# Gate steps between the halves of up steps, a gate evacuation in six VectorE steps, and two gaps between tiles

## The chip, the cores and the metric

The kernel runs on one core of one Trainium2 chip. The metric is the device time of one execution in microseconds. The median of three timed runs is 2343.71 us (2341.99 to 2345.11); the execution that was profiled took 2340.65 us.

## The reference

Two decoder layers over 256 positions of width 2048 in float32, and a final RMSNorm. Each layer runs four groups of attention heads, adds their merged projection, and then the dense SwiGLU block, in which the change lies:

```python
for l in range(DEPTH):                                   # DEPTH = 2
    x = x + hybrid_mixer(rms_norm(x, attn_norm[l]), w_in[l], ...)
    h = rms_norm(x, ffn_norm[l])                         # 256 x 2048
    x = x + (jax.nn.silu(h @ w_gate[l]) * (h @ w_up[l])) @ w_down[l]   # hidden width 5632
return rms_norm(x, final_norm)
```

## The kernel before

**Numbers.** float32 operands are split into a high part, rounded to the type that TensorE takes at full rate, and the rest. A product is then three matmuls: high x high, high x rest, rest x high. `XS[i]` holds both parts of the normed x (two of the sixteen row blocks of 128 each), `wh` and `wl` those of the weights. `load` (L230) takes one unit of weights, 128 x 2048, from HBM into `raw` (one DMA on SP's queue, three buffers), and splits it in two halves of 1024 columns: ScalarE writes `wh` (L239), VectorE subtracts it to `wl` (L240). There are six buffers of `wh` and six of `wl`, each of 1024 columns.

**A layer's feed-forward part** runs over eleven blocks `g` of 512 hidden columns. `gate_up(g)` makes four steps for up and four for gate, in turns: u0 g0 u1 g1 u2 g2 u3 g3, each over a quarter of the 2048 rows and with one unit of weights. An up step (`ProjV.step`) is 24 matmuls of 512 columns at L256, x stationary, weights moving, into one of the two accumulators of the pool `accp` (`acc`, two banks of PSUM each). In block 0 the gate is a `ProjV` as well and takes the other accumulator. In blocks 1 to 10 the gate is a `ProjSW`: seven products in place of eight, from sums of the weights' quarters (`w_sum`, L350 to L355 on VectorE, split at L354, L356 to L358) and sums of x (`sums`, built once a layer, in the pool `qp`). Such a step is 42 matmuls of 256 columns (L371 to L373) and uses four pairs of the weight buffers; its seven results lie in the four banks of the pool `attp` (`att`). `out` (L375) adds them up: one step on ScalarE and seven on VectorE. Then Silu on ScalarE (L802; L798 in block 0) and, on VectorE, the product with up (L803), which is the last reader of up's accumulator.

**Around a block.** `turn` transposes the block's hidden values on TensorE (L813) through two `att` banks into `h` tiles. `down(c, p)` multiplies eight of these tiles by 256 columns of `w_down` (16 x a matmul of 512 columns and one of 256) in an accumulator and adds the result to X in two VectorE steps (`add_to`, L281 and L282), the second of which frees the accumulator. Blocks 0 and 1 have no down projections behind them, blocks 2 to 9 have four, block 10 has eight. `turn` of an even block comes in the program after the first of them, of an odd one after the last; of blocks 0 and 1 after the first up step of the block that follows.

**Order.** The program gives each engine's instructions; a planner orders them with its own durations, so VectorE's and ScalarE's steps of several units lie mixed, and `tc.issue_after` is the means to hold an order.

**Addresses.** `GAP_X`, `GAP_W`, `GAP_H` and `GAP_Q` are dead tiles, of so many times 32 bytes of each partition, ahead of `XS`, the weight buffers, the `h` tiles and the pool `qp`.

Of the kernel before, what the change touches and what calls it, by code (L numbers as in the profile page):

```python
# [8 lines left out]
F32 = mybir.dt.float32  # L9
# [6 lines left out]
S = 256  # L16
# [12 lines left out]
NG = HID // 512  # L29
GAP_X, GAP_W, GAP_H, GAP_Q = 1, 3, 1, 1  # L30

# [85 lines left out]
def pack_weights(w_in, w_uq, w_ukv, w_out, w_gate, w_up, w_down):  # L117
    us = []
    for l in range(DEPTH):
# [39 lines left out]
        for g in range(NG):  # L159
            for i in range(4):  # L160
                us += [up(g, i), unit(w_gate[l], 4 * i, 4, 0, 512) if g == 0 else gate(g, i)]
            for c, ps in down_after(g):
                us += dn(8 * c, 8, ps)
# [19 lines left out]
def trunk(ctx: ExitStack, tc: tile.TileContext, x_d, w_d, sm_d, c_d, out_d):  # L183
# [124 lines left out]
    class ProjV:  # L308
        def __init__(self, src, nk):
            self.acc, self.src, self.nk = Acc(), src, nk  # L310
            self.out = [self.acc.t[:, t].rearrange("p a b -> p (a b)") for t in range(2)]

        def step(self, k0):
            blk = load()
            for kk in range(4):
                x = self.src(k0 + kk)
                wh, wl = blk(kk * 512, 512)
                last = k0 + kk == self.nk - 1
                for t in range(2):
                    ts = slice(t * 128, t * 128 + 128)  # L320
                    self.acc.mm(t, self.out[t], x[:, 0, ts], wh, False)
                    self.acc.mm(t, self.out[t], x[:, 0, ts], wl, False)
                    self.acc.mm(t, self.out[t], x[:, 1, ts], wh, last)
# [7 lines left out]
    class ProjSW:  # L331
# [3 lines left out]
        def banks(self):  # L335
            ps = [attp.tile([128, 2, S], F32, name="att") for _ in range(4)]
            self.p = {1: ps[0][:, 0], 2: ps[0][:, 1], 3: ps[1][:, 0], 6: ps[2][:, 0],
                      7: ps[2][:, 1], 5: ps[3][:, 0], 4: ps[3][:, 1]}

        def step(self, k0):  # L340
# [3 lines left out]
            for j in range(2):  # L344
# [14 lines left out]
                a, b = slice(0, 128), slice(128, 256)  # L359
                x, y = XS[i], self.sums[i]  # L360
                for n, xh, xl, wh, wl, o in (
# [4 lines left out]
                        (7, y[:, 2, 0, :], y[:, 2, 1, :], ht, lt, 256),  # L366
                        (5, y[:, 0, 0, :], y[:, 0, 1, :], ht, lt, 0),
                        (4, x[:, 1, 0, b], x[:, 1, 1, b], ht, lt, 768)):
                    p, c = self.p[n], slice(o, o + 256)
                    first = i == 0 and n in (1, 3, 6, 5)  # L370
                    P.matmul(p, xh, wh[:, c], start=first, stop=False, skip_group_check=True)  # L371
                    P.matmul(p, xl, wh[:, c], start=False, stop=False, skip_group_check=True)  # L372
                    P.matmul(p, xh, wl[:, c], start=False, stop=i == 7, skip_group_check=True)  # L373

        def out(self):  # L375
            p = self.p
            c = [tp.tile([128, 512], F32, name="ff_g", tag="t2", bufs=T2) for _ in range(2)]
            c11, c12, c21, c22 = c[0][:, :256], c[0][:, 256:], c[1][:, :256], c[1][:, 256:]
            A.activation(c11, p[1], AF.Copy)
            V.tensor_add(c12, c11, p[6])  # L380
            V.tensor_add(c11, c11, p[2])
            V.tensor_add(c21, c12, p[7])
            V.tensor_sub(c12, c12, p[5])
            V.tensor_add(c12, c12, p[3])
            V.tensor_sub(c22, c21, p[5])
            V.tensor_add(c21, c21, p[4])
            return c
# [178 lines left out]
    for l in range(DEPTH):  # L566
# [214 lines left out]
        def gate_up(g, turn_last):  # L781
            up = ProjV(xk, KT)
            gate = ProjV(xk, KT) if g == 0 else ProjSW(sums)
            for i in range(4):
                up.step(4 * i)
                if i == 0 and turn_last is not None:
                    turn_last()
                gate.step(4 * i)
            if g == 0:
# [94 lines left out]
```

## Time and profile before

| | |
|---|---|
| median of three runs | 2343.71 us |
| profiled execution | 2340.65 us |
| its span, first to last instruction | 2338.8 us |
| TensorE busy | 2256.6 us, 96% |
| VectorE busy | 1834.7 us, 78% |
| ScalarE busy | 1256.3 us, 54% |
| up steps, v and block 0's gate (weights over x) at L256 | 2880 matmuls of 512 columns |
| gate steps of blocks 1 to 10 at L371 to L373 | 3360 matmuls of 256 columns |

Matmuls overlap: the duration of one holds a tail that runs beside the next one, so the rate is read from the time of a number of matmuls, or from differences of durations of one shape. In the names, `acc<-wh,XS` is a matmul into `acc` with `wh` moving and `XS` stationary. PEclk is the granted clock as a share of 2.4 GHz.

### The profile page before, as it was taken

What the parts mean: (1) busy time and instruction counts of PE and PEld (TensorE: products, weight loads), DVE (VectorE), ACT (ScalarE), POOL (GpSimd) and SP (SyncE); (2) the same over time, 40 slices, a digit from 0 to 9 for tenths busy, and PEclk for the clock granted to TensorE, in tenths of its full rate; (3) what the DMA queues carried; (4) which work ended last, traced back from release to release, by engine and by line L of the source; (5) the groups of instructions that cost most, each with busy time, mean ns of one, the idle gap of its engine ahead of it and who ended that gap; (6) DMA issues with size and microseconds to landing.
All of it is one profiled execution on the core that took longest, in us unless ns stands there. A gap on an engine that the chain in (4) does not pass through costs nothing.

```text
span 2338.8 us, 34343 instructions
## 1 busy us (share of the span) xinstructions
PE 2256.6 (96%) x13678; PEld 2007.8 (86%) x13678; DVE 1834.7 (78%) x2639; ACT 1256.3 (54%) x1629; POOL 0.2 (0%) x4
## 2 busy tenths in 40 slices
PE   8999999999999999999999999999999999999997
PEld 8888889788888888888998988897888888888887
DVE  8876767798888888778877865778887888887775
ACT  7454556654455544445564654666644445544454
POOL 0000000000000000000000000000000000000000
PEclk9999999999999999999999999999999999999999
DMA  7544445455455455455555344454544455444452
GB/s 294 185 151 178 154 149 206 159 192 187 180 198 198 172 178 186 168 187 198 186 184 189 138 168 158 166 202 159 190 172 180 179 198 198 171 172 174 174 209 90
DMA packets 61648, 419.88 MB, mean 180 GB/s; under 512 B 6832, under 2 KB 7088, under 8 KB 14768
## 3 DMA queue, kind: packets, MB, share of 16 engines
q1 hardware_dynamic: 61344, 417.63, 49.7%
q8 instruction: 107, 1.75, 0.3%
q14 instruction: 53, 0.43, 0.0%
q10 hardware_dynamic: 144, 0.07, 0.0%
HBM read 415.57 MB, written 2.10 MB: 179 GB/s over the span
## 4 chain that ended last, share of the span: by engine, by line
PE 93%; DVE 3%; ACT 2%; DMA 1%; issue 0%; ACTq 0%; DVEq 0%; SPq 0%
PE acc L256 70%; PE att L373 5%; PE att L371 5%; PE att L372 5%; PE att L256 4%; DVE wl L240 1%; ACT wh L239 1%; PE att L813 1%; DMA raw<-in_w_dram 1%; PE att L494 1%; DVE X L282 0%; PE att L484 0%; PE att L495 0%; PE att L503 0%; DMA X<-in_x_dram 0%
## 5 line engine op out<-in xcount | busy, mean ns | idle before, releaser
L239 ACT ACTIVATE wh<-raw 128x1024 fp32r<-128x1024 f32 (+1 forms) x650 | 663.6, 1027 | 744.2 <-PE acc L256 600.9
L240 DVE TENSOR_TENSOR wl<-raw,wh 128x1024 fp32r<-128x1024 f32 (+1 forms) x650 | 764.8, 1183 | 317.8 <-ACT wh L239 312.2
L256 PE MATMUL acc<-h,wh 128*128 128x512 f32 (+1 forms) x1824 | 629.1, 390 | 52.1 <-DVE X L282 52.1
L256 PE MATMUL acc<-wh,XS 128*128 128x512 f32 x1920 | 620.9, 397 | 8.4 <-ACT ff_g L798 8.4
L256 PE MATMUL acc<-h,wl 128*128 128x256 f32 x1744 | 499.9, 287 | 0.0
L256 PEld LDWEIGHTS acc<-h,wh 128*128 128x128 f32 x1824 | 345.6, 192 | 123.7 <-issue 53.4
L256 PEld LDWEIGHTS acc<-wh,XS 128*128 128x128 f32 x1920 | 362.5, 189 | 92.1 <-ACT ff_g L798 8.5
L256 PE MATMUL acc<-XS,wh 128*128 128x512 f32 (+1 forms) x1344 | 376.6, 347 | 6.3 <-ACT XS L435 6.3
L256 PE MATMUL acc<-wl,XS 128*128 128x512 f32 x960 | 381.1, 397 | 1.0 <-DVE wl L240 1.0
L256 PEld LDWEIGHTS acc<-h,wl 128*128 128x128 f32 x1744 | 337.8, 194 | 0.2
L256 PE MATMUL acc<-XS,wl 128*128 128x256 f32 x1056 | 299.1, 283 | 0.0
L256 PEld LDWEIGHTS acc<-XS,wh 128*128 128x128 f32 x1344 | 233.6, 189 | 38.8 <-ACT XS L435 6.3
L357 ACT ACTIVATE wh<-w_sum 128x1024 fp32r<-128x1024 f32 x160 | 169.8, 1061 | 143.3 <-PE acc L256 70.0
L358 DVE TENSOR_TENSOR wl<-w_sum,wh 128x1024 fp32r<-128x1024 f32 x160 | 195.7, 1223 | 38.6 <-ACT wh L357 29.9
L256 PEld LDWEIGHTS acc<-wl,XS 128*128 128x128 f32 x960 | 181.6, 189 | 41.8 <-DVE wl L240 1.8
L256 PEld LDWEIGHTS acc<-XS,wl 128*128 128x128 f32 x1056 | 199.1, 189 | 0.8
L371 PE MATMUL att<-wh,xs_sum 128*128 128x256 f32 x640 | 178.5, 279 | 0.0
L373 PE MATMUL att<-wl,xs_sum 128*128 128x256 f32 x640 | 178.5, 279 | 0.0
L372 PE MATMUL att<-wh,xs_sum 128*128 128x256 f32 x640 | 178.5, 279 | 0.0
L354 ACT ACTIVATE wh<-raw 128x768 fp32r<-128x768 f32 x160 | 134.4, 840 | 69.4 <-PE acc L256 61.1
L356 DVE TENSOR_TENSOR wl<-raw,wh 128x768 fp32r<-128x768 f32 x160 | 152.4, 953 | 23.4 <-ACT wh L354 23.4
L371 PE MATMUL att<-wh,XS 128*128 128x256 f32 x480 | 134.6, 280 | 0.0
(188 smaller groups left out, 2620.6 us busy)
## 6 DMA issues: line engine op xcount, KB each, us to landing
raw<-in_w_dram SPq DMA_DIRECT2D x364, 1024.0 KB, 4.8
raw<-in_w_dram SPq DMA_DIRECT2D x32, 768.0 KB, 4.4
raw<-in_w_dram SPq DMA_DIRECT2D x8, 512.0 KB, 6.8
X<-in_x_dram SPq DMA_DIRECT2D x8, 256.0 KB, 6.1
out_dram<-X SPq DMA_DIRECT2D x8, 256.0 KB, 2.4
cst<-in_const_dram SPq DMA_DIRECT2D x1, 1216.0 KB, 8.7
raw<-in_w_dram SPq DMA_DIRECT2D x4, 256.0 KB, 5.0
cst<-in_const_dram SPq DMA_DIRECT2D x1, 67.0 KB, 7.1
```

What stands on the lines that cost most here:

```text
L239: A.activation(wh[:, i:e], raw[:, o + i:o + e], AF.Copy)
L240: V.tensor_sub(wl[:, i:e], raw[:, o + i:o + e], wh[:, i:e].bitcast(F32))
L256: P.matmul(out, lhsT, rhs, start=bank not in self.started, stop=stop, skip_group_check=True)
L354: A.activation(hs[:, :768], q[:, :768], AF.Copy)
L356: V.tensor_sub(ls[:, :768], q[:, :768], hs[:, :768].bitcast(F32))
L357: A.activation(ht, t, AF.Copy)
L358: V.tensor_sub(lt, t, ht.bitcast(F32))
L371: P.matmul(p, xh, wh[:, c], start=first, stop=False, skip_group_check=True)
L372: P.matmul(p, xl, wh[:, c], start=False, stop=False, skip_group_check=True)
L373: P.matmul(p, xh, wl[:, c], start=False, stop=i == 7, skip_group_check=True)
L494: P.matmul(po[:, :S], vt[0][:, hs], p[:, :S], start=True, stop=False, skip_group_check=True)
L813: P.transpose(pt[:, f, t * 128:t * 128 + 128], hid[t][:, (2 * p + f) * 128:(2 * p + f + 1) * 128], ident)
```

## The change

The steps of a block run in the order of `STEPS`: u0 g0 u1 g1 u2 g2 g3 u3. An up step is cut into halves of two row blocks (12 matmuls) each; the gate step that follows runs between them, and u3 runs whole at the end. `turn` of the block before, where it is still due, comes behind the first half of u0. Block 0's gate takes two `att` banks in place of an accumulator. The seven results of a gate lie in the four banks in another arrangement, so that products 2 and 6 are side by side and `out` adds product 1 to both in one VectorE step of 512 columns; there are six VectorE steps in place of seven. `issue_after` keeps the first matmul of the second product of a bank behind that of the first. `pack_weights` puts the units into the new order. `GAP_W` goes from 3 to 5 and `GAP_Q` from 1 to 7.

```diff
--- before.py
+++ after.py
@@ -1,4 +1,4 @@
-from contextlib import ExitStack
+from contextlib import ExitStack, nullcontext
 
 import numpy as np
 import concourse.bass as bass
@@ -27,7 +27,8 @@
 LINE = 8
 RAW_B, W_B, H_B, Q_B4, T2, SG = 3, 6, 7, 8, 3, 3
 NG = HID // 512
-GAP_X, GAP_W, GAP_H, GAP_Q = 1, 3, 1, 1
+GAP_X, GAP_W, GAP_H, GAP_Q = 1, 5, 1, 7
+STEPS = ("u0", "g0", "u1", "g1", "u2", "g2", "g3", "u3")
 
 Q_LAT, KV_LAT, K_ROPE = 0, 512, 1024
 Q_B, K_B, V_B = 1088, 1600, 2112
@@ -157,8 +158,12 @@
             return [unit(w_down[l], k0, n, c0 * cols, cols) for c0 in ps]
 
         for g in range(NG):
-            for i in range(4):
-                us += [up(g, i), unit(w_gate[l], 4 * i, 4, 0, 512) if g == 0 else gate(g, i)]
+            for what in STEPS:
+                i = int(what[1])
+                if what[0] == "u":
+                    us.append(up(g, i))
+                else:
+                    us.append(unit(w_gate[l], 4 * i, 4, 0, 512) if g == 0 else gate(g, i))
             for c, ps in down_after(g):
                 us += dn(8 * c, 8, ps)
         us += dn(8 * (NG // 2), 4, range(4))
@@ -306,13 +311,17 @@
         return acc.t
 
     class ProjV:
-        def __init__(self, src, nk):
-            self.acc, self.src, self.nk = Acc(), src, nk
-            self.out = [self.acc.t[:, t].rearrange("p a b -> p (a b)") for t in range(2)]
+        def __init__(self, src, nk, out=None):
+            self.acc, self.src, self.nk = Acc(out), src, nk
+            self.out = out or [self.acc.t[:, t].rearrange("p a b -> p (a b)") for t in range(2)]
 
         def step(self, k0):
             blk = load()
-            for kk in range(4):
+            self.half(k0, blk, 0)
+            self.half(k0, blk, 2)
+
+        def half(self, k0, blk, k1):
+            for kk in range(k1, k1 + 2):
                 x = self.src(k0 + kk)
                 wh, wl = blk(kk * 512, 512)
                 last = k0 + kk == self.nk - 1
@@ -334,8 +343,9 @@
 
         def banks(self):
             ps = [attp.tile([128, 2, S], F32, name="att") for _ in range(4)]
-            self.p = {1: ps[0][:, 0], 2: ps[0][:, 1], 3: ps[1][:, 0], 6: ps[2][:, 0],
-                      7: ps[2][:, 1], 5: ps[3][:, 0], 4: ps[3][:, 1]}
+            self.p = {2: ps[0][:, 0], 6: ps[0][:, 1], 1: ps[1][:, 0], 7: ps[2][:, 0],
+                      4: ps[2][:, 1], 5: ps[3][:, 0], 3: ps[3][:, 1]}
+            self.p26 = ps[0]
 
         def step(self, k0):
             if self.p is None:
@@ -357,33 +367,36 @@
                 A.activation(ht, t, AF.Copy)
                 V.tensor_sub(lt, t, ht.bitcast(F32))
                 a, b = slice(0, 128), slice(128, 256)
-                x, y = XS[i], self.sums[i]
+                x, y, opened = XS[i], self.sums[i], {}
                 for n, xh, xl, wh, wl, o in (
                         (1, x[:, 0, 0, a], x[:, 0, 1, a], hs, ls, 0),
                         (2, x[:, 1, 0, a], x[:, 1, 1, a], hs, ls, 512),
                         (3, y[:, 3, 0, :], y[:, 3, 1, :], hs, ls, 256),
                         (6, y[:, 1, 0, :], y[:, 1, 1, :], ht, lt, 512),
                         (7, y[:, 2, 0, :], y[:, 2, 1, :], ht, lt, 256),
-                        (5, y[:, 0, 0, :], y[:, 0, 1, :], ht, lt, 0),
-                        (4, x[:, 1, 0, b], x[:, 1, 1, b], ht, lt, 768)):
+                        (4, x[:, 1, 0, b], x[:, 1, 1, b], ht, lt, 768),
+                        (5, y[:, 0, 0, :], y[:, 0, 1, :], ht, lt, 0)):
                     p, c = self.p[n], slice(o, o + 256)
-                    first = i == 0 and n in (1, 3, 6, 5)
-                    P.matmul(p, xh, wh[:, c], start=first, stop=False, skip_group_check=True)
+                    first = i == 0 and n in (1, 2, 3, 7)
+                    lead = {6: 2, 4: 7, 5: 3}.get(n) if i == 0 else None
+                    with tc.issue_after(opened[lead]) if lead else nullcontext():
+                        opened[n] = P.matmul(p, xh, wh[:, c], start=first, stop=False,
+                                             skip_group_check=True).ins
                     P.matmul(p, xl, wh[:, c], start=False, stop=False, skip_group_check=True)
                     P.matmul(p, xh, wl[:, c], start=False, stop=i == 7, skip_group_check=True)
 
         def out(self):
             p = self.p
             c = [tp.tile([128, 512], F32, name="ff_g", tag="t2", bufs=T2) for _ in range(2)]
-            c11, c12, c21, c22 = c[0][:, :256], c[0][:, 256:], c[1][:, :256], c[1][:, 256:]
-            A.activation(c11, p[1], AF.Copy)
-            V.tensor_add(c12, c11, p[6])
-            V.tensor_add(c11, c11, p[2])
-            V.tensor_add(c21, c12, p[7])
+            c12, c21, c22 = c[0][:, 256:], c[1][:, :256], c[1][:, 256:]
+            one = tp.tile([128, S], F32, name="p1", tag="sg", bufs=SG)
+            A.activation(one, p[1], AF.Copy)
+            V.tensor_add(c[0].rearrange("p (a b) -> p a b", a=2), b2(one), self.p26)
+            V.tensor_add(c22, c12, p[7])
             V.tensor_sub(c12, c12, p[5])
             V.tensor_add(c12, c12, p[3])
-            V.tensor_sub(c22, c21, p[5])
-            V.tensor_add(c21, c21, p[4])
+            V.tensor_add(c21, c22, p[4])
+            V.tensor_sub(c22, c22, p[5])
             return c
 
     def sumsq(srcs):
@@ -780,12 +793,23 @@
 
         def gate_up(g, turn_last):
             up = ProjV(xk, KT)
-            gate = ProjV(xk, KT) if g == 0 else ProjSW(sums)
-            for i in range(4):
-                up.step(4 * i)
-                if i == 0 and turn_last is not None:
-                    turn_last()
-                gate.step(4 * i)
+            if g == 0:
+                gate = ProjV(xk, KT, [attp.tile([128, 512], F32, name="att") for _ in range(2)])
+            else:
+                gate = ProjSW(sums)
+            for n, what in enumerate(STEPS):
+                k0 = 4 * int(what[1])
+                if what[0] == "u":
+                    blk = load()
+                    up.half(k0, blk, 0)
+                    if n == 0 and turn_last is not None:
+                        turn_last()
+                    if n == len(STEPS) - 1:
+                        up.half(k0, blk, 2)
+                else:
+                    gate.step(k0)
+                    if STEPS[n - 1][0] == "u":
+                        up.half(k0, blk, 2)
             if g == 0:
                 rc.append(rcol(rf, "rxc"))
                 rc.append(tp.tile([128, 2], F32, name="rfn", bufs=1))
```

## Rows read from the trace of the kernel before

**Rows 1.** The page's head: the span, and busy time of each engine.

```profile
span 2338.8 us, 34343 instructions
...
PE 2256.6 (96%) x13678; PEld 2007.8 (86%) x13678; DVE 1834.7 (78%) x2639; ACT 1256.3 (54%) x1629; POOL 0.2 (0%) x4
```

**Rows 2.** Waits of TensorE: who waited for whom, total us, times, longest us.

```profile
PE acc L256 <- DVE X L282: 52.1, 18, 3.2
PE acc L256 <- ACT ff_g L798: 8.4, 2, 4.2
```

**Rows 3.** Timeline of TensorE, 611 to 621 us: start, us, line, operation, operands.

```profile
611.16 0.28 PE L373 MATMUL att<-wl,XS 128*128 128x256 f32 x1
...
616.72 0.28 PE L256 MATMUL acc<-h,wl 128*128 128x256 f32 x1
620.03 0.47 PE L256 MATMUL acc<-h,wh 128*128 128x512 f32 x1 [3.04 <-DVE X L282]
```

**Rows 4.** Timeline of VectorE, 611 to 622 us.

```profile
611.13 0.41 DVE L380 TENSOR_TENSOR ff_g<-ff_g,att 128x256 f32<-128x256 f32 x1
...
616.76 0.41 DVE L386 TENSOR_TENSOR ff_g<-ff_g,att 128x256 f32<-128x256 f32 x1
617.09 0.68 DVE L281 TENSOR_TENSOR X<-X,acc 128x512 f32<-128x512 f32 x1
618.07 1.23 DVE L240 TENSOR_TENSOR wl<-raw,wh 128x1024 fp32r<-128x1024 f32 x1 [0.30 <-ACT wh L239]
...
619.81 1.40 DVE L803 SCALAR_TENSOR_TENSOR ff_g<-acc,rxc,ff_g 128x512 f32<-128x512 f32 x2
```

**Rows 5.** Timeline of all engines, 446 to 456 us: block 0 to block 1.

```profile
451.69 1.26 ACT L798 ACTIVATE ff_g<-acc,rxc 128x512 f32<-128x512 f32 x2
...
453.01 0.80 PE L256 MATMUL acc<-wh,XS 128*128 128x512 f32 x1 [4.18 <-ACT ff_g L798]
```

**Rows 6.** Stretches: us, busy by engine (PE to POOL), PEclk, DMA share, GB/s.

```profile
448.57:453.02 4.45, 0.27 (x4) 0.18 (x3) 3.08 (x9) 4.42 (x7) 0.00 (x0) 0.76 0.63 232
453.02:457.75 4.73, 4.73 (x11) 3.77 (x12) 4.03 (x11) 1.08 (x2) 0.00 (x0) 0.50 0.00 0
...
620.03:625.55 5.52, 5.51 (x32) 4.88 (x33) 4.95 (x9) 1.06 (x1) 0.00 (x0) 1.00 0.53 190
...
957.10:960.60 3.50, 0.33 (x2) 0.01 (x1) 3.50 (x7) 1.85 (x3) 0.00 (x0) 0.84 0.58 246
960.60:966.30 5.70, 5.64 (x17) 4.85 (x18) 3.78 (x8) 0.31 (x1) 0.00 (x0) 0.50 0.57 184
...
2325.00:2338.80 13.80, 0.56 (x3) 0.15 (x1) 6.60 (x12) 3.71 (x5) 0.00 (x0) 0.62 0.41 152
```

**Rows 7.** Cores: span and mean granted clock.

```profile
core 0: 2338.8 us, clock 0.986
```

**Rows 8.** Stretches: a step pair, an up step, a gate step, another gate step.

```profile
579.83:590.37 10.54, 10.54 (x67) 9.46 (x67) 9.10 (x13) 5.83 (x7) 0.00 (x0) 1.00 0.54 196
...
590.20:595.79 5.59, 5.59 (x26) 4.52 (x25) 5.21 (x8) 2.13 (x2) 0.00 (x0) 1.00 0.78 311
595.79:600.74 4.95, 4.95 (x43) 4.94 (x42) 3.89 (x6) 3.70 (x4) 0.00 (x0) 1.00 0.25 68
...
674.65:679.41 4.76, 4.76 (x43) 4.71 (x42) 3.80 (x5) 4.40 (x6) 0.00 (x0) 1.00 0.29 86
```

**Rows 9.** Stretch: the first down projection behind a block.

```profile
611.28:616.84 5.56, 5.56 (x34) 4.81 (x32) 5.42 (x10) 3.06 (x4) 0.00 (x0) 1.00 0.94 373
```

**Rows 10.** Operations on acc: count, ns min/median/max, first and last start.

```profile
L256 PE MATMUL acc<-wh,XS x1920: 388/394/796, 105.3 to 2248.1; 128*128 128x512 f32 x192
...
L256 PE MATMUL acc<-h,wh x1824: 277/390/763, 130.2 to 2300.1; 128*128 128x512 f32 x167, 128*128 128x256 f32 x16
...
L256 PE MATMUL acc<-wh,h x32: 392/396/476, 148.2 to 1307.0; 128*128 128x512 f32 x32
```

## The prediction

> **What bounds the kernel now.** I read the page's head first: TensorE is busy for 96% of a span of 2338.8 us, VectorE for 78%, ScalarE for 54% [rows 1]. So time is won in two ways only: TensorE stands still less, or the same matmuls run at a higher rate. The profiled execution took 2340.65 us; the median of the three timed runs is 2343.71, which is 3.1 us more, and I carry those 3.1 us to the end.
>
> Standing still: the waits of TensorE have two large entries, 52.1 us in 18 waits for `add_to`'s second addition (L282), and 8.4 us in 2 waits for the Silu of block 0 (L798) [rows 2]. All other entries together are under 10 us. The timeline shows the first kind: the first down projection after a gate/up block ends at 616.72 + 0.28 us, and the next one starts at 620.03 [rows 3]. Both PSUM accumulators are taken then. One is that of the down projection just ended, which `add_to` must read; the other still holds the up projection of the block, which L803 reads last. VectorE shows why neither is free: the gate's last matmul ran at 611.16 [rows 3], but the seven steps of `out` lie between weight splits from 611.13 to 617.17 us, and L803 comes at 619.81 [rows 4]. The up product has been ready for it since before the gate's last step began. The eighteen waits are blocks 2 to 10 of both layers. The second kind is block 0, where gate and up hold one accumulator each, so the next up step waits until 453.01 us for the two Silus [rows 5].
>
> What follows a wait costs too: the granted clock is 0.50 after the wait of block 0, and again after the one at 957 us; after the wait that ended at 620.03 us it is 1.00 [rows 6]. The mean over the span is 0.986 [rows 7], so 2338.8 x 0.014 x 2 = 65 us ran at the lower level (1.2 GHz). 10.5 us of these lie in the tail of the kernel [rows 6], and about 6.5 us inside the waits themselves (2.1 us in each of the two of block 0, 1.1 us in each of the two like 957 us), so some 48 us of matmuls ran at half rate: a loss of 24 us.
>
> Rate: 24 wide matmuls of an up step take 5.59 us (233 ns each; 512 columns at 2.4 GHz are 213), the 42 of a gate step 4.95 us (118 ns) in one block and 4.76 us (113 ns) in another, for 107 at 2.4 GHz [rows 8]. Of the twenty blocks whose gate runs in seven products, twelve go like the former and eight like the latter.
>
> **The change, part by part.**
>
> *Up ends last.* After the change the gate's last matmul is followed by a whole up step of 5.59 us [rows 8], and then by the first down projection, 5.56 us [rows 9]. The accumulator of up is needed 11.15 us after the gate ends. In these VectorE must run `out` (one step of 512 columns, 0.69 us as L281 of the same size, and five of 0.41: 2.76 us), L803 twice (1.40 us) and four weight splits of two units to come (4 x 1.22 us): 9.0 us [rows 4]. ScalarE's four Silus start under the up step. So L803 ends before the first down projection does, with some 2 us to spare, and the second finds an accumulator: the 52.1 us go. If the splits get ahead of L803 in VectorE's queue, what is late next is the same accumulator; the price is then at most the wait of today, 2.9 us a block.
>
> *Block 0's gate in other banks.* Its product now lies in two of the four `att` banks, so one accumulator is free at once for block 1: the 8.4 us go. But the turn of block 0 and the seven products of block 1 want those banks as well. I bound that from both sides by 0 and by the old wait, 4.2 us, at each of four places (blocks 0 and 1 of two layers, which have no down projections behind them), and take 1 us each: 4 us.
>
> *The clock.* With no wait of 3 us left, nothing in the trace of before brings the clock down in these stages: 24 us. It goes with the waits, so it is lost again if they return.
>
> *Gate steps between halves of up steps.* The matmuls are the same. The second half of an up step keeps its pair of weight buffers through the gate step between (4.95 us), so five pairs are left to go round in that time instead of six. VectorE has work for 9.10 us of a pair of steps of 10.54 us [rows 8], so it still keeps ahead on the mean. At the end g2 and g3 have only half an up step (2.8 us) between them: VectorE needs 9.10 us less two splits of 1.22, so 6.7 us, for a gate step's sums and splits, and has 2.8 + 4.95 us from the start of g2 until g3 starts, and some further 2.5 us until its second half is needed. I cost it at nothing for that cover, and at up to 1 us a block (20 us) if VectorE is behind there.
>
> *Six VectorE steps.* One step of 0.69 us replaces two of 0.41 [rows 4]: 0.1 us a block, 3 us of VectorE in all, none of it on the path. The sequence of banks is changed, the number of matmuls isn't.
>
> *Distances.* From the sizes in the code (rows of a tile rounded up to 32 bytes), `XS` and the weights lie 69312 bytes apart before, 64 short of a multiple of 256; the weights and `q` (with the sums) 77888, 64 over one. Afterwards both are multiples of 256. `h` stays 32 bytes over one. No matmul of note at a distance of zero is in the trace, so I bound it by the nearest. Weights streaming over `XS` (before: -64) have a median of 394 ns, `h` over weights (+32) 390, weights over `h` (-32) 396 [rows 10]. The matmul's own tail is in all three, so the differences are those of rate. If zero goes like +32, the 2880 wide up and v matmuls win 4 ns each (11.5 us), and if the twelve slow gate blocks become like the fast ones, 12 x 168 x 4.5 ns = 9 us more: -21 us. If it goes one such step the other way (+4 ns wide, +5 ns on 3360 gate matmuls), +28 us. Zero lies as near to the 390 as to the 396, but two gate rates exist at one distance, which leaves more to win than to lose; I take -8 us and keep both ends.
>
> Here a page speaks against the last part. The Trainium skill, TensorE: Matmul & The Clock Gate, Part 2 (Step-by-step), says that TensorE has a read port each for the moving and the stationary operand and that "Loading the next tile's weights doesn't steal SBUF read bandwidth from the running matmul." By that the distance is worth 0 us and the sum would be 8 us higher. The trace doesn't fit it well (390 against 394 and 396 ns for one shape), but what moves differs between these rows too.
>
> The sum: 2340.65 - 52.1 - 8.4 - 24 + 4 - 8 = 2252 us, and with the 3.1 us to the median 2255.
>
> **The rivals.** (a) *The waits come back in part*: L803 behind splits, the banks at blocks 0 and 1, or g3 waiting for its splits. For it: VectorE's slack is only 2 us in 11. Against: it isn't late at the first gate step of a block now. Half of the 84.5 us lost again gives about 2297 us. (b) *Zero is the bad distance*: the moving rows and the rows that are loaded beside them then start at like addresses, and whatever makes 390 into 396 ns may be at its worst there. +28 us instead of -8 gives 2291. (c) *Zero takes nearly all of the stretch away*: 233 to 213 ns over 2880 and 116 to 107 ns over 3360 matmuls are at most 87 us; half of that in place of the 8 gives 2220. (d) *Slower than before*: the up half that is held starves the gate steps of buffers. There are 80 such gate steps, each behind the half step that came out of its cover; VectorE has 1.4 us to spare per pair of steps [rows 8]. From 88 / 80 = 1.1 us of wait a step the win is eaten, and waits of that length may bring the clock down again; at 1.5 us it is about 2375. (e) *The order doesn't move*: the planner places VectorE's steps by its own times, so L803 could stay where it is. Then only block 0 and the distances act: about 2320.
>
> **How the numbers follow.** Forecast 0.56 (its own range 2238 to 2274), (a) 0.14, (b) 0.11, (c) 0.09, (d) 0.06, (e) 0.04. The range reaches from (c) to (e): 2222 to 2312 leaves out (d) and halves of (c) and (e), and the worse ends of (a), some 2 in 10. What a measurement of this kernel can tell from no change is about 0.2%, 4.7 us. Faster: all of the forecast, (b) and (c), most of (a) and (e): 0.89; same 0.03; slower 0.08.
>
> **What the profile after would show.** Right: the entry of L282 gone from TensorE's waits, L803 done before the first down projection ends, the clock at 1.00 from the first block to the last, `out` under the last up step. For the distances: an up step of 24 matmuls at 5.5 us or less, gate steps at 4.76 us throughout. Wrong: new waits of TensorE for L240 or L358 at gate steps (d), for `att` banks at blocks 1 and 2, up steps above 5.7 us (b). The prediction is wrong as a whole if the second down projection of a block still starts 3 us late.

## The result, and the profile after

| | before | after |
|---|---|---|
| median, same comparison | 2342.85 us (2337.88 to 2345.11, 4 runs) | 2263.01 us (2261.55 to 2264.44, 4 runs) |
| ratio after / before, 95% interval | | 0.9662 (0.9645 to 0.9679) |
| profiled execution | 2340.65 us | 2263.72 us |

The kernel is 3.4% faster. The forecast was 2255 us: the direction and the main cause held, and 8 us of the gain did not come. The lines of the changed kernel are L245 for the split into `wl`, L261 for `Acc`'s matmul, L286 and L287 for `add_to`, L385 for gate matmuls, L393 to L399 for `out`, L827 for the product with up and L837 for `turn`.

The page's head and the cores' view of after answer to [rows 1, 7]:

```profile
span 2261.9 us, 34303 instructions
...
PE 2235.6 (99%) x13678; PEld 2009.5 (89%) x13678; DVE 1829.5 (81%) x2619; ACT 1222.5 (54%) x1605; POOL 0.2 (0%) x4
...
core 0: 2261.9 us, clock 0.996
```

TensorE went from 96% busy to 99%. Its waits, as in [rows 2] (who waited for whom, total us, times, longest us):

```profile
PE acc L261 <- ACT XS L448: 6.3, 1, 6.3
PE att L837 <- DVE ff_g L827: 4.1, 4, 2.1
PE acc L261 <- DVE wl L245: 3.6, 2, 1.8
```

Both large entries are gone, that of `add_to` and that of block 0's Silu. The first line is a wait at the kernel's start that before has too. The second is new, and the third, for the weight split, was 1.0 us in before. They are the subject of experiments e6, e7 and e11.

The stretches of after (columns as in [rows 6]) that answer to [rows 8, 9]: a gate step g3, the up step u3 behind it, the first down projection, the second one, and then 560 us at once:

```profile
595.34:600.38 5.04, 5.04 (x44) 5.04 (x43) 3.71 (x4) 4.34 (x5) 0.00 (x0) 1.00 0.39 140
600.38:605.84 5.46, 5.46 (x26) 4.51 (x25) 5.44 (x9) 3.32 (x5) 0.00 (x0) 1.00 0.94 375
605.84:611.41 5.57, 5.57 (x33) 4.91 (x32) 4.04 (x5) 2.52 (x3) 0.00 (x0) 1.00 0.66 241
611.41:616.95 5.54, 5.54 (x35) 4.94 (x34) 5.30 (x8) 2.12 (x2) 0.00 (x0) 1.00 0.48 174
560.00:1120.00 560.00, 560.00 (x3466) 505.87 (x3465) 476.23 (x621) 297.99 (x337) 0.00 (x0) 1.00 0.54 194
```

Behind the first down projection `turn` starts at 611.41 and the second one at 611.55, where before TensorE stood still for 3 us [rows 3]. From 560 to 1120 us TensorE doesn't stop once, and the granted clock is 1.00. An up step of 24 matmuls went from 5.59 to 5.46 us, a gate step of 42 from 4.95 or 4.76 to 5.04 [rows 8].

The timeline of VectorE in after, around that u3, answers to [rows 4]:

```profile
600.17 0.68 DVE L394 TENSOR_TENSOR ff_g<-p,att 128x512 f32<-128x512 f32 x1
...
605.61 0.41 DVE L399 TENSOR_TENSOR ff_g<-ff_g,att 128x256 f32<-128x256 f32 x1
606.11 0.75 DVE L827 SCALAR_TENSOR_TENSOR ff_g<-acc,rxc,ff_g 128x512 f32<-128x512 f32 x1
...
608.34 0.74 DVE L827 SCALAR_TENSOR_TENSOR ff_g<-acc,rxc,ff_g 128x512 f32<-128x512 f32 x1
...
611.61 0.69 DVE L286 TENSOR_TENSOR X<-X,acc 128x512 f32<-128x512 f32 x1 [0.53 <-PE acc L261]
```

`out` runs from 600.17 to 606.02 us, beside u3 (600.38 to 605.84). L827 ends at 609.08 and lets go of up's accumulator; `turn` needs its result at 611.41, and the second down projection the accumulator at 611.55: 2.3 us to spare in this block. `add_to`'s first addition now waits for TensorE instead of the other way round.

### The profile page after: what moved, and what is told of

Same layout as the page of the kernel before. It is cut to its first block, busy times and chain, and to the rows that moved or that the text cites. A ratio compares the mean times of both kernels' runs of the same rounds, so it can differ in the third digit from the quotient of the medians.

```text
span 2261.9 us, 34303 instructions
## 1 busy us (share of the span) xinstructions
PE 2235.6 (99%) x13678; PEld 2009.5 (89%) x13678; DVE 1829.5 (81%) x2619; ACT 1222.5 (54%) x1605; POOL 0.2 (0%) x4
## 4 chain that ended last, share of the span: by engine, by line
PE 95%; DVE 2%; ACT 1%; DMA 1%; issue 1%; DVEq 0%; SPq 0%; ACTq 0%
PE acc L261 68%; PE att L261 6%; PE att L385 6%; PE att L383 6%; PE att L386 6%; PE att L837 1%; PE att L507 1%; DVE wl L245 1%; DMA raw<-in_w_dram 0%; PE att L497 0%; PE att L508 0%; PE att L516 0%; ACT wh L367 0%; DVE wl L366 0%; DVE wl L368 0%
## 5 line engine op out<-in xcount | busy, mean ns | idle before, releaser
L245 DVE TENSOR_TENSOR wl<-raw,wh 128x1024 fp32r<-128x1024 f32 (+1 forms) x650 | 764.1, 1182 | 252.6 <-ACT wh L244 249.4
L261 PE MATMUL acc<-h,wh 128*128 128x512 f32 (+1 forms) x1824 | 615.4, 384 | 0.0
L261 PE MATMUL acc<-wh,XS 128*128 128x512 f32 x1792 | 570.4, 390 | 0.1
L261 PE MATMUL acc<-h,wl 128*128 128x256 f32 x1744 | 493.5, 283 | 0.0
L261 PEld LDWEIGHTS acc<-wh,XS 128*128 128x128 f32 x1792 | 336.8, 188 | 69.5 <-ACT wh L244 1.0
L261 PEld LDWEIGHTS acc<-h,wh 128*128 128x128 f32 x1824 | 338.6, 189 | 64.6
L261 PE MATMUL acc<-XS,wh 128*128 128x512 f32 (+1 forms) x1344 | 379.6, 350 | 6.3 <-ACT XS L448 6.3
L261 PE MATMUL acc<-wl,XS 128*128 128x512 f32 x896 | 350.0, 391 | 3.6 <-DVE wl L245 3.6
L261 PEld LDWEIGHTS acc<-h,wl 128*128 128x128 f32 x1744 | 330.7, 190 | 1.0
L261 PE MATMUL acc<-XS,wl 128*128 128x256 f32 x1056 | 300.2, 284 | 0.0
L261 PEld LDWEIGHTS acc<-XS,wh 128*128 128x128 f32 x1344 | 236.1, 191 | 38.4 <-ACT XS L448 6.3
L261 PEld LDWEIGHTS acc<-XS,wl 128*128 128x128 f32 x1056 | 201.6, 191 | 0.8
L261 PEld LDWEIGHTS acc<-wl,XS 128*128 128x128 f32 x896 | 168.5, 188 | 35.6 <-DVE wl L245 4.4
L385 PE MATMUL att<-wh,xs_sum 128*128 128x256 f32 x640 | 179.0, 283 | 0.0
```

What stands on the lines that cost most here:

```text
L245: V.tensor_sub(wl[:, i:e], raw[:, o + i:o + e], wh[:, i:e].bitcast(F32))
L261: P.matmul(out, lhsT, rhs, start=bank not in self.started, stop=stop, skip_group_check=True)
```

## The experiments

All kernels below but e2 are the changed kernel with the edit named. Times are medians in us, with the lowest and highest run. The runs of before spread from 2333 to 2353 us from one execution to the next (the spread goes with the clock, see the last section), those of the other kernels by 1 to 8 us. So two versions of the changed kernel are compared by their own medians. Line numbers shift with the edits: the product with up is L827 in after, L822 in e6 and L823 in e11, and `turn` is L837, L832 and L833.

| | edit | median | ratio to before (95%) |
|---|---|---|---|
| after | | 2263.01 (2261.55 to 2264.44) | 0.9662 (0.9645 to 0.9679) |
| e5 | whole up steps, gate last | 2331.43 (2327.28 to 2335.30) | 0.9934 (0.9914 to 0.9955) |
| e4 | halves, g3 ahead of half of u3 | 2263.33 (2263.07 to 2265.76) | 0.9662 (0.9629 to 0.9694) |
| e6 | whole up steps, up last | 2259.59 (2258.14 to 2262.06) | 0.9631 (0.9613 to 0.9650) |
| e7 | block 0's gate in an accumulator | 2267.93 (2267.03 to 2268.82) | 0.9664 (0.9649 to 0.9679) |
| e11 | seven steps, old banks | 2255.87 (2255.34 to 2256.01) | 0.9629 (0.9595 to 0.9663) |
| e1 | old gaps | 2267.60 (2267.25 to 2268.38) | 0.9681 (0.9653 to 0.9708) |
| e2 | before, new gaps | 2333.95 (2330.91 to 2339.15) | 0.9963 (0.9947 to 0.9978) |
| e3 | `GAP_Q` 1 | 2258.95 (2256.72 to 2260.23) | 0.9642 (0.9615 to 0.9670) |
| e8 | `GAP_W` 6, `GAP_Q` 6 | 2269.92 (2269.39 to 2271.04) | 0.9673 (0.9658 to 0.9688) |
| e9 | e6 with `GAP_Q` 1 | 2256.44 (2256.13 to 2257.04) | 0.9632 (0.9599 to 0.9666) |
| e10 | e6 with `GAP_Q` 3 | 2257.59 (2257.36 to 2258.29) | 0.9638 (0.9597 to 0.9678) |
| e12 | e9 with a later `turn` | 2257.53 (2256.68 to 2257.92) | 0.9636 (0.9602 to 0.9670) |

### Which step ends a block: e5, e6, e4

e6 takes the halves out, and e5 besides puts the last gate step behind the last up step:

```diff
-STEPS = ("u0", "g0", "u1", "g1", "u2", "g2", "g3", "u3")
+STEPS = ("u0", "g0", "u1", "g1", "u2", "g2", "u3", "g3")      # e5 only
...
-                    blk = load()
-                    up.half(k0, blk, 0)
+                    up.step(k0)
...
-                    if n == len(STEPS) - 1:
-                        up.half(k0, blk, 2)
...
-                    if STEPS[n - 1][0] == "u":
-                        up.half(k0, blk, 2)
```

e5: 

> The changed kernel with whole steps in the order of before, u0 g0 u1 g1 u2 g2 u3 g3, nothing behind the gate; gaps, six VectorE steps, banks and block 0's gate as changed. Theory (what lies behind the gate's last step is what takes the 18 waits away): L282 is back in TensorE's waits with about 52 us, and the clock falls again behind some of them (10 to 20 us): 2320 to 2335. Rival (the six VectorE steps and the new banks shorten the evacuation enough): under 20 us of waits, below 2290.

e6: 

> The changed kernel with whole up steps (u0 g0 u1 g1 u2 g2 g3 u3), so that only the halves are undone. Theory (the prediction costs the halves at nothing): 2263 within 5. Rival 1 (the halves are what keeps the weight splits ahead of the gate steps, above all between g2 and g3, which then follow each other with the whole of u2 ahead of them): waits for L240, L366 or L368 of 1 us or more a block, 2285 or more. Rival 2 (the halves hold a pair of buffers and cost something): a few us faster, 2255.

Waits of TensorE in e5, then in e6:

```profile
PE acc L261 <- DVE X L287: 55.7, 18, 3.6
```

```profile
PE att L832 <- DVE ff_g L822: 3.7, 4, 1.8
PE acc L261 <- DVE wl L245: 3.5, 2, 1.8
```

With the gate last, all eighteen waits are back, though the gate's banks, the six steps and the gaps are the new ones. Between e5 and e6 nothing but the order of u3 and g3 differs, and that is worth 71.8 us: 55.7 us of waits, and the clock. e5's mean granted clock is 0.992 over 2325.4 us and e6's 0.998 over 2256.8, which makes 37 and 9 us at 1.2 GHz, and half the difference is 14 us. This one exchange is nine tenths of what the whole change wins.

e4 is the changed kernel with e5's `STEPS`. With the halves kept, half of u3 (12 matmuls) then runs behind g3.

> The changed kernel with the steps in the order u0 g0 u1 g1 u2 g2 u3 g3, halves kept: the gate step g3 lies between the halves of u3, and half an up step (2.8 us) is the last. Up's accumulator is then needed 8.4 us after the gate ends, and VectorE has 9.0 us of work for it by the prediction's count. Theory (the cover that a whole up step gives is what takes the waits away): waits for the accumulator come back in part, 0.6 us or more a block, 2270 to 2300. Rival (half a step is cover enough, what counts is that anything lies behind the gate): 2263 within 5.

It takes the same time as after. VectorE and TensorE in e4, where the half step ends at 605.27 us:

```profile
610.43 0.74 DVE L827 SCALAR_TENSOR_TENSOR ff_g<-acc,rxc,ff_g 128x512 f32<-128x512 f32 x1
```

```profile
611.23 0.50 PE L261 MATMUL acc<-h,wh 128*128 128x512 f32 x1
```

The last L827 ends at 611.17 and the second down projection starts at 611.23, with a `turn` ahead of it. So half an up step behind the gate is just enough cover, with nothing to spare in this block.

e6 against after is the price of the halves: 3.4 us less without them, and 2.5 us between e9 and e3, which have `GAP_Q` 1 both. The ranges overlap in both pairs. The halves win nothing; that they cost about 0.1% is likely, but not clear of the scatter. Starvation of the gate steps, rival (d), is in no profile: TensorE has no entry for the gate's weights.

### Block 0's gate: e7

```diff
-                gate = ProjV(xk, KT, [attp.tile([128, 512], F32, name="att") for _ in range(2)])
+                gate = ProjV(xk, KT)
```

> The changed kernel with block 0's gate in the second accumulator, as before. Theory: block 1 waits for an accumulator until block 0 has been read; since up now ends last the Silus can start earlier, but L827 must follow for up's own one, or the Silu for the gate's: 2 to 4.4 us of wait in each of two layers, and the lower clock behind them (2 to 3.4 us each): 2269 to 2278. Rival (the up step that now ends last covers the reading, the other banks are worth nothing): 2263 within 4.

Waits of TensorE in e7:

```profile
PE acc L261 <- ACT ff_g L822: 8.4, 2, 4.2
...
PE att L837 <- DVE ff_g L827: 3.3, 4, 1.4
```

The 8.4 us are those of before [rows 2]. But the 3.6 us for L245, which after has, are not there, and the wait for L827 is 0.8 us shorter. So the two `att` banks for block 0's gate win 4.9 us by the medians, not the 8.4 us of the wait: what is taken away between blocks 0 and 1 comes back in part one block later.

### The gate's PSUM and its six steps: e11

e11 has the whole class `ProjSW` of before in the changed kernel: bank arrangement, order of the products, `out` in seven steps, and no `issue_after`.

```diff
-            self.p = {2: ps[0][:, 0], 6: ps[0][:, 1], 1: ps[1][:, 0], 7: ps[2][:, 0],
-                      4: ps[2][:, 1], 5: ps[3][:, 0], 3: ps[3][:, 1]}
+            self.p = {1: ps[0][:, 0], 2: ps[0][:, 1], 3: ps[1][:, 0], 6: ps[2][:, 0],
+                      7: ps[2][:, 1], 5: ps[3][:, 0], 4: ps[3][:, 1]}
...
-                    with tc.issue_after(opened[lead]) if lead else nullcontext():
-                        opened[n] = P.matmul(p, xh, wh[:, c], start=first, stop=False,
-                                             skip_group_check=True).ins
+                    P.matmul(p, xh, wh[:, c], start=first, stop=False, skip_group_check=True)
...
-            V.tensor_add(c[0].rearrange("p (a b) -> p a b", a=2), b2(one), self.p26)
+            V.tensor_add(c12, c11, p[6])
+            V.tensor_add(c11, c11, p[2])
```

> The changed kernel with the gate's product class of before: seven VectorE steps, the old arrangement of the seven results in the four banks, the old order of products 4 and 5 and no held order within a bank. Theory (the prediction costs the six steps at nothing on the path): 2263 within 4, gate matmuls at 120 ns as in the changed kernel. Rival 1 (VectorE's queue is tight behind a block, so 0.1 us and one instruction more bring waits for L827 back): 2270 or more. Rival 2 (the sequence of banks is what slows the gate to 120 ns): gate at 116, 2250.

It is 7.1 us faster than after, with ranges that are far apart. Neither theory had that. The waits of TensorE in e11:

```profile
PE att L833 <- DVE ff_g L823: 0.9, 4, 0.2
...
PE acc L261 <- ACT wh L244: 0.6, 1, 0.6
```

The two new waits of after have all but gone: 1.5 us in place of 7.7. The stretches in which they lie, blocks 0 to 2 of each layer, in after and then in e11:

```profile
440.00:560.00 120.00, 115.81 (x697) 103.03 (x696) 104.33 (x157) 67.51 (x85) 0.00 (x0) 0.99 0.52 185
1560.00:1680.00 120.00, 116.43 (x701) 103.48 (x701) 105.06 (x157) 67.00 (x86) 0.00 (x0) 0.99 0.51 184
```

```profile
440.00:500.00 60.00, 59.95 (x363) 53.34 (x362) 56.92 (x93) 38.88 (x50) 0.00 (x0) 1.00 0.50 176
500.00:560.00 60.00, 59.54 (x368) 53.30 (x368) 52.62 (x74) 32.13 (x38) 0.00 (x0) 1.00 0.55 198
1560.00:1680.00 120.00, 118.92 (x742) 106.82 (x742) 110.16 (x163) 71.15 (x86) 0.00 (x0) 1.00 0.51 186
```

In after TensorE is idle for 4.2 and 3.6 us of these 240 us, in e11 for 0.5 and 1.1. These 6.2 us are most of the difference of the spans (2261.9 against 2254.2 us). The clock comes on top: 0.996 and 0.998 are 18 and 9 us at the lower level, half the difference some 4 us. Together that is some 3 us more than the difference, for which no row accounts. VectorE's timeline at the end of block 1 shows the lateness, first in after, then in e11:

```profile
487.96 0.68 DVE L394 TENSOR_TENSOR ff_g<-p,att 128x512 f32<-128x512 f32 x1
...
493.30 0.41 DVE L399 TENSOR_TENSOR ff_g<-ff_g,att 128x256 f32<-128x256 f32 x1
...
497.67 1.22 DVE L245 TENSOR_TENSOR wl<-raw,wh 128x1024 fp32r<-128x1024 f32 x1
...
499.14 1.40 DVE L827 SCALAR_TENSOR_TENSOR ff_g<-acc,rxc,ff_g 128x512 f32<-128x512 f32 x2
```

```profile
486.54 0.41 DVE L389 TENSOR_TENSOR ff_g<-ff_g,att 128x256 f32<-128x256 f32 x1
...
490.74 0.42 DVE L395 TENSOR_TENSOR ff_g<-ff_g,att 128x256 f32<-128x256 f32 x1
...
494.81 1.41 DVE L823 SCALAR_TENSOR_TENSOR ff_g<-acc,rxc,ff_g 128x512 f32<-128x512 f32 x2
```

Both kernels start block 1's gate within 0.4 us of each other. `out` ends 2.6 us later in after, and the product with up comes 4.3 us later. The weight split at 497.67 is what TensorE waits for at the start of block 2 (its timeline in after):

```profile
496.55 0.61 PE L261 MATMUL acc<-wh,XS 128*128 128x512 f32 x2
498.95 0.50 PE L261 MATMUL acc<-wl,XS 128*128 128x512 f32 x1 [1.78 <-DVE wl L245]
```

VectorE was late before `out` began: the four weight splits ahead of it end at 488.0 us in after and at 485.4 in e11. So the time of the wide step is not the cause. VectorE stood still in the first gate step of block 1, and again in that of block 2, each time for a split that ScalarE had to write first. VectorE in after:

```profile
460.78 0.96 DVE L366 TENSOR_TENSOR wl<-raw,wh 128x768 fp32r<-128x768 f32 x1 [2.02 <-ACT wh L364]
463.66 1.23 DVE L368 TENSOR_TENSOR wl<-w_sum,wh 128x1024 fp32r<-128x1024 f32 x1 [1.93 <-ACT wh L367]
...
509.42 1.23 DVE L368 TENSOR_TENSOR wl<-w_sum,wh 128x1024 fp32r<-128x1024 f32 x1 [3.94 <-ACT wh L367]
```

In e11 VectorE waits no longer than 0.39 us in that step of block 1 and 0.90 us in that of block 2. The first split that ScalarE writes there, in after and then in e11:

```profile
459.90 0.85 ACT L364 ACTIVATE wh<-raw 128x768 fp32r<-128x768 f32 x1 [2.18 <-issue]
```

```profile
455.15 0.85 ACT L363 ACTIVATE wh<-raw 128x768 fp32r<-128x768 f32 x1 [0.66 <-PE att L381]
```

In e11 a gate matmul releases it, in after it comes 4.7 us later. The code suggests why. There are four `att` banks. `turn` of the block before holds two of them until its result is read, and the gate's first 18 matmuls go to the other two. In the old arrangement these hold products 1, 2 and 3, which are all that read the split of the weights themselves, so its buffer comes free. In the new one they hold 1, 2 and 6, so that this buffer and that of the sums both stay in use. So the trace points to the arrangement of the banks. No run changes it alone, and what the order held by `issue_after` and the planner's order add stays open.

### A later turn: e12

e12 is e9 with `turn` of an even block behind the second down projection instead of the first, to give L827 more time.

```diff
-                if n == (0 if g % 2 == 0 else len(todo) - 1):
+                if n == (1 if g % 2 == 0 else len(todo) - 1):
```

> As e9, with the turn of even blocks after the second down projection instead of the first. In the changed kernel TensorE's last waits for a block's hidden values are those of block 2, 2.1 us once a layer, because its turn stands in TensorE's queue ahead of the second down projection. Theory: these waits go (3.7 to 5 us in all) and with them a fall of the clock: 4 to 7 us below e9. Rival (the second down projection then waits in the turn's place, since the accumulator hangs on the same L827, or the wait moves on): e9 within 2.

Nothing is won. TensorE's wait at `turn` is 3.1 us in all where e9 has 3.3, and 2257.53 us is 1.1 us above e9. The rival held: TensorE still waits behind the first down projection, in layer 0 for 1.69 us ahead of `turn` and 0.22 us for the accumulator. Both hang on the same product with up (L822), wherever `turn` stands.

### The distances: e1, e2, e3, e8, e9, e10

```diff
-GAP_X, GAP_W, GAP_H, GAP_Q = 1, 5, 1, 7
+GAP_X, GAP_W, GAP_H, GAP_Q = 1, 3, 1, 1      # e1;  e3: 1, 5, 1, 1;  e8: 1, 6, 1, 6
```

By the sizes in the code the distance of x and the weights, modulo 256 bytes, is -64 in e1, 0 in after and e3, +32 in e8; that of the weights and the sums is +64 in e1 and e3, 0 in after, -32 in e8, 128 in e10.

e1: 

> The changed kernel with the four gaps of before (1, 3, 1, 1): the new order and evacuation alone. In the changed kernel the up matmuls came down from 233 to 228 ns (2880 of them: -15 us), and the gate matmuls went up from 116 to 120 ns (3360: +13 us). Theory: the 77 us come from the waits and the clock alone and the gaps nearly cancel; then this run is at 2263 us within 5, with up at 233 and the gate at 113 to 118 ns. Rival 1: the distances won the 15 us and the gate became slower through the new order or the new banks: about 2278, with the gate still at 120 ns. Rival 2: the gaps cost more than they won: about 2250.

e2, the kernel before with the gaps 1, 5, 1, 7: 

> The kernel before with the new gaps (1, 5, 1, 7) and nothing else. Theory: the waits of L282 stay at about 52 us and the clock at 0.986; up goes to 228 ns and the gate to 120, and the time stays within 5 us of 2343. Rival 1 (the gate's 120 ns are of the banks or the order): up 228 and the gate still 113 to 118, about 2328. Rival 2 (the distance acts on neither): nothing moves.

e3: 

> The changed kernel with GAP_Q back at 1: x stays a multiple of 256 bytes from the weights, the sums of x go back to 64 over one. Theory (each matmul's rate hangs on the distance of its own two operands): the 1920 gate matmuls over sums go back from 120 to 116 ns, the 1440 over x stay at 120, up stays at 228: -7.7 us, about 2255. Rival 1 (the whole gate step falls into one rate): all 3360 go back to 113 to 118: about 2250. Rival 2 (order or banks set the gate's rate): 2263, nothing moves.

e8: 

> The changed kernel with gaps 1, 6, 1, 6: the weights 32 bytes above a multiple of 256 from x, and as far from the sums, the distance at which h over weights runs (229 ns for 512 columns and 117 to 118 for 256). Theory (the rate is a matter of moving minus stationary address, whatever the tiles): up at about 229 ns instead of 228 (+3 us), gate at 114 to 118 ns instead of 120 (-7 to -20 us), x over weights in the q and k projections now at -32 (2 us either way): 2245 to 2258. Rival (zero is the special distance, the others are alike): up back at 233 and gate at 117, 2268, as with the old gaps.

e9: 

> The changed kernel with whole up steps (as e6) and GAP_Q at 1 (as e3): the two single edits that made the changed kernel faster, by 3.4 and 4.1 us. Theory (they act on different things, steps on the order and the clock, the gap on the rate of 1920 gate matmuls): they add, 2263.0 - 7.5 = 2255.5 within 3. Rival (both were faster because the clock fell once rather than three times, so the same gain was counted twice): 2259 to 2260.

e10: 

> As e9, with GAP_Q at 3: the sums 128 bytes over a multiple of 256 from the weights. Theory (only at a distance of zero do all 256-column matmuls fall into the slow rate of 120 ns): gate matmuls over sums at 116 to 118 ns, as at 64 and at 32, and the time of e9 within 3. Rival (the rate follows the distance step by step): a rate outside 113.5 to 119, and 3 us or more away from e9.

Operations by tile (count, ns min/median/max, first and last start), up steps over x and gate matmuls over the sums: after, e1, e3, e8, and e10.

```profile
L261 PE MATMUL acc<-wh,XS x1792: 387/389/507, 107.8 to 2179.9; 128*128 128x512 f32 x200
...
L385 PE MATMUL att<-wh,xs_sum x640: 278/283/285, 455.1 to 2174.4; 128*128 128x256 f32 x160
```

```profile
L261 PE MATMUL acc<-wh,XS x1792: 388/394/498, 105.3 to 2183.5; 128*128 128x512 f32 x200
...
L385 PE MATMUL att<-wh,xs_sum x640: 276/281/286, 455.9 to 2177.9; 128*128 128x256 f32 x160
```

```profile
L261 PE MATMUL acc<-wh,XS x1792: 387/389/497, 107.5 to 2172.9; 128*128 128x512 f32 x200
...
L385 PE MATMUL att<-wh,xs_sum x640: 276/281/287, 454.4 to 2167.4; 128*128 128x256 f32 x160
```

```profile
L261 PE MATMUL acc<-wh,XS x1792: 388/394/505, 106.5 to 2186.4; 128*128 128x512 f32 x200
...
L385 PE MATMUL att<-wh,xs_sum x640: 277/278/282, 457.2 to 2180.8; 128*128 128x256 f32 x160
```

```profile
L385 PE MATMUL att<-wh,xs_sum x640: 274/280/290, 454.1 to 2168.3; 128*128 128x256 f32 x160
```

Of the distances tried, zero is the best for matmuls of 512 columns (389 ns against 394 on both sides) and the worst for those of 256 (283 against 278 to 281). The distance alone does not set the rate: at +32 the weights over x take 394 ns in e8, and `h` over weights, also at +32, 390 [rows 10]. From the starts of the same matmuls in the traces the means are 233.1 ns in e1 and 227.8 in after for the 2880 wide ones, 117.2 and 119.95 for the 1920 gate matmuls over sums, 117.3 and 119.55 for the 1440 over x. That is 15.3 us won and 5.3 + 3.2 us lost, and with some 2 us lost in matmuls of the first stages it is a gain of 4.8 us; the medians of e1 and after say 4.6. Undoing the sums' part alone (e3) wins 4.1 us more. With whole steps e9 wins 3.2 us over e6, so the two edits nearly add up.

e2 wins 8.9 us on the kernel before, more than its rates give. Its waits are the same 52.1 us in 18, but its clock is 0.992 where the profile of before had 0.986 [rows 7]: 37 against 65 us at the lower level. This is not the scatter of single runs: in the same comparison the ten runs of e2 have clocks of 0.989 to 0.993, and the thirteen of before 0.983 to 0.988. Why the clock falls less behind the same waits when the gaps differ stays open.

e11 at 2255.87 and e9 at 2256.44 us are the fastest kernels that ran. e11's class with whole steps and `GAP_Q` 1 was not run.

## Why the prediction was right or wrong

**Up ends last: right, in mechanism and size.** 52.1 us were forecast from this. The entry is gone, and e5, which against e6 undoes it alone, brings back 55.7. The cover was forecast with some 2 us to spare and has 2.3. A whole step was taken as needed, and e4 shows that half of one does.

**The clock: right in kind, somewhat large.** 24 us were taken for matmuls at half rate. After runs 2261.9 x 0.004 x 2 = 18 us at the lower level in place of 65. Taking 6.5 us inside the old waits off, that is 40 us of work at full rate again, or 20 us. The 4 us that are missing are falls behind the new waits: "nothing in the trace of before brings the clock down in these stages" did not reckon with them.

**Block 0's banks: half right.** The 8.4 us went. The 4 us put against them stood for the `att` banks at blocks 0 and 1. The waits that came are 4.1 and 3.6 us (the latter 1.0 before), for VectorE's split and product one and two blocks later. TensorE doesn't wait for a bank there, but the trace of e11 leads back to the banks that `turn` and the gate share, as the prediction feared, by way of the weight buffers.

**Six VectorE steps: the part that failed.** They were costed at nothing, since they take 3 us off VectorE, and of the banks it was said only that their sequence changes and the number of matmuls does not. VectorE's load was not the question: with the class undone (e11) the kernel is 7.1 us faster and 6.2 of the 7.7 us of new waits go. The sum of durations was right. What was left out is which products can run while `turn` holds two banks, and so when a weight buffer comes free; that this is the cause is read from the trace and the code, and not tested alone. The prediction had looked at the cover of blocks that have down projections behind them; the loss starts at blocks 1 and 2, where `turn` falls into the gate's first step.

**Halves: not nothing, but near.** By the medians they cost 3.4 us (e6) or 2.5 (e9 against e3), with ranges that overlap. The price goes with the clock more than with waits: e6 has 7.2 us of waits where after has 7.7, but 9 us at the lower level in place of 18.

**Distances: mis-sized, and wrong in kind.** -8 us was taken, with ends of -21 and +28 for all matmuls going one way. They went two ways, and the gaps by themselves are worth 4.6 us (e1). The wide matmuls gave more than the better end had for them (15.3 us for 11.5), the gate matmuls lost; rival (b) holds for one shape and the forecast for the other. Against the kernel before the gate lost still more: the eight blocks that went at the fast rate there (means of 113.3 and 117.8 ns a matmul over sums) do so in no block of after, and in only three of twenty of e1, whose gaps are the old ones. So another part of the change took that rate away. By rates of before and after the term is -15.3 + 12.8 + 2 = -0.5 us.

The Trainium skill, TensorE: Matmul & The Clock Gate, Part 2 (Step-by-step), says that loading the next weights takes no read bandwidth from the running matmul, by which a distance is worth nothing. The runs don't agree with a worth of nothing: e1 and after differ in the dead tiles alone, and the same matmuls take 394 and 389 ns, or 281 and 283. Whether the read of the weights is the cause is not shown.

The difference of 11.7 us between the sum for the profiled execution (2252) and its time (2263.72) is then 2.7 of waits (7.7 us, less the 4 allowed for and the 1.0 of before), 4 of clock and 7.5 of distances, less 2.5 that no row accounts for. The median of after lies 0.7 us under its profiled run, where 3.1 above it was carried over from before. That leaves the 8 us. These last 3.8 us are scatter: it is luck that they bring the forecast nearer.

## What to carry to other kernels

Ask of each PSUM accumulator who reads it last and what runs on TensorE until it is needed: putting the operand with the long evacuation chain first, and a step of other matmuls behind it, won 72 us here without fewer matmuls, and half a step was enough in e4. An edit that only saves steps on an engine with time to spare can still cost: where banks are short, their arrangement decides which products run first and, as the trace suggests here, when operand buffers come free. Look for it at the stages with the least cover, which are the first blocks of a layer here. When addresses are moved, measure each shape of matmul by itself: one distance was the best of those tried for 512 columns and the worst for 256.

## What the runs showed of the hardware that was not expected

**Distance and shape.** For the rates by distance see e1 to e10: with 512 columns 227.8 ns at zero and 233.1 at -64 and +32, with 256 columns (over the sums) 119.95 at zero and 116.8 to 118.0 at -32, +64 and 128. Why the shapes differ is open.

**The clock falls after some short waits and not after others.** `turn` of block 2 in after (timeline of TensorE), first in layer 0 and then in layer 1, and behind them the same place of layer 0 in e6:

```profile
544.21 0.44 PE L837 MATMUL att<-cst,ff_g 128*128 128x128 f32 x2 [2.13 <-DVE ff_g L827]
...
1662.88 0.44 PE L837 MATMUL att<-cst,ff_g 128*128 128x128 f32 x2 [1.52 <-DVE ff_g L827]
```

```profile
542.66 0.44 PE L832 MATMUL att<-cst,ff_g 128*128 128x128 f32 x2 [1.79 <-DVE ff_g L822]
```

The stretches behind them, two of after and one of e6:

```profile
546.06:550.00 3.94, 3.94 (x19) 3.44 (x18) 3.55 (x7) 0.94 (x2) 0.00 (x0) 0.71 0.80 262
1664.80:1668.80 4.00, 4.00 (x16) 3.42 (x16) 3.48 (x7) 0.49 (x2) 0.00 (x0) 0.62 0.70 262
```

```profile
546.00:550.00 4.00, 4.00 (x25) 3.56 (x24) 4.00 (x9) 1.33 (x2) 0.00 (x0) 1.00 0.56 229
```

The granted clock fell to 1.2 GHz for part of the stretch after waits of 2.13 and 1.52 us, and stayed at 2.4 GHz after one of 1.79. In e3 it was 1.00 from 500 to 600 us, with a wait of 2.4 us at that place. So the length of the wait alone doesn't decide it. The same holds for the waits of 3 us: before and e2 have the same eighteen, with mean clocks of 0.986 and 0.992, and runs of before spread over 20 us. A kernel that keeps TensorE busy gets rid of that scatter as well: e11's runs lie within 0.7 us.
